# Three small moves of order and engine in a one-core decoder layer: a turn's copies, a unit's scores, a round's sums of weights

## The chip, the cores and the metric

The kernel runs on one core of a Trainium2 chip. The metric is the device time of one execution in microseconds (us). In the text PE is TensorE, DVE is VectorE, ACT is ScalarE, POOL is GpSimd, and SP is the engine that issues most DMAs. PEld stands for the loads of weights into PE, which overlap its products. L705 is line 705 of the kernel before.

## The reference

One decoder layer over 512 tokens of width 1024, in fp32:

```python
x = x + 0.5 * swiglu(rms_norm(x, g_ffn1), w_ffn1_gate, w_ffn1_up, w_ffn1_down)
proj = rms_norm(x, g_mix) @ w_in             # q, k, v, conv input u, memory queries mq
y_attn = sliding_window_attention(...)       # 8 heads, window 128, per-head sinks
y_conv = conformer_conv(...)                 # GLU, causal depthwise conv of 31 taps, LayerNorm, swish
y_mem  = memory_cross_attention(...)         # 4 heads into 256 memory tokens
x = x + concat(y_attn, y_conv, y_mem) @ w_out
x = x + 0.5 * swiglu(rms_norm(x, g_ffn2), w_ffn2_gate, w_ffn2_up, w_ffn2_down)
```

with `swiglu(x, wg, wu, wd) = (silu(x @ wg) * (x @ wu)) @ wd` and 2816 hidden columns.

## The kernel before

Activations lie transposed, channels on the 128 partitions and the 512 tokens along the free axis. Every product with weights is made of three products of parts in fp32r: high times high, low times high, high times low. So each weight tile is loaded as fp32 by SP (`wraw`), split into a high part by an ACT cast (L208, L214) and a low part by a DVE subtraction (L209, L219). The class `Weights` keeps that queue in order: `split_to(n)` makes all items up to n, `four(i)` makes the sums of one weight tile.

The layer has three stages: the first feed-forward block (to about 360 us), the mixing stage with attention, convolution and memory (to about 510 us), and the second feed-forward block. Most of the feed-forward products use a seven-product scheme (Strassen-Winograd) on halves of 256 tokens, which needs sums of weight blocks: `four` computes four sums of 128x256 each with four DVE instructions (L147 to L150).

**Mixing.** The steps are written in a list, `ORDER`. The six attention units are M0, M1 (memory) and S0 to S3 (window), each of two heads. For each unit: `scores?0` and `scores?1` (products of q and k into two `sc` or two `mm` banks of PSUM, L1161), `soft?j` (masked maxima on DVE, L1179, exponentials on ACT, L1197), `weights?` (division by the sums, split over DVE, L1217, and ACT, L1219), `turn?h` (for a window unit seven PE transposes, L1232, in groups of four and three into two `tp` banks, and a copy of each group to SBUF, L1235, by ACT), and `values?` (L1246), whose result is split into yh and yl (L1262, L1263). `c` is one pair of convolution taps on DVE (L1089). `out{d}_{ks}` adds products of the output projection for column block d (L421 to L423). `ln_mean`, `ln_square` and `ln_var` are the LayerNorm of the convolution (L1351 to L1376), `ln_swish` its end (L1382, L1383). A planner orders the instructions of each engine from modelled times, with the order of the program as priority; on the chip each engine then works through its own order and waits where an operand isn't there. There are four `mm`, two `sc` and two `tp` banks, handed out as they come free.

**Last down round.** It is the one stage in which PE, DVE and ACT keep the order of the program exactly. `seven(g)` does columns 2g and 2g+1 of the output for g = 0 to 3, with two weight items each: `wa` (the raw tile, three quarters) and `ws` (the four sums). The halves of results are taken from PSUM by ACT (`half`, L530), added into x (by a POOL DMA with accumulation for g = 0, L590, by DVE from there on, L588) and the finished columns are written by `leave` (L598: one DVE operation, then an output DMA, L601). `leave` for quarter g runs in quarter g+1. `ahead` prepares the weights of the next quarters. For g < 2 it is called after the product T1, for g > 1 at the beginning of the quarter. For g = 1 it makes the second item of quarter 2 and the sums for quarter 3.

Of the kernel before, what the change touches and what calls it, by code (L numbers as in the profile page):

```python
# [67 lines left out]
pS0 ropeS0 pS1 sumA facA ropeS1 c valuesM1 pS2 scoresS01 scoresS00 softS00 softS01 c weightsS0 ropeS2 c  # L68
pS3 scoresS10 softS10 scoresS11 out0_01 sumB facB c turnS00 turnS01 softS11 scoresS20 c weightsS1 c c
valuesS0 turnS10 scoresS21 out1_01 softS20 out1_2 ropeS3 softS21 c c turnS11 weightsS2 c valuesS1 scoresS30  # L70
turnS20 out0_2 scoresS31 softS31 turnS21 softS30 out1_3 out2_0123 weightsS3 c c out0_3 valuesS2 c c out3_0123 c
c ln_mean ln_square turnS30 ln_var out4_0123 turnS31 out5_0123 valuesS3
""".split()
TILES = [s[1:] for s in ORDER if s[0] == "p"]
# [202 lines left out]
def layer(tc, ctx, a):  # L277
    nc = tc.nc
    PE, ACT, DVE, POOL = nc.tensor, nc.scalar, nc.vector, nc.gpsimd
# [12 lines left out]
    def mm_bank():  # L292
        return psum.tile([P, T], F32, tag="mm", name=nm("mm"), bufs=4)

    def sc_bank():
        return psum.tile([P, T], F32, tag="sc", name=nm("sc"), bufs=2)
# [4 lines left out]
    def work():  # L301
        return tmp.tile([P, T], F32, tag="t", name=nm("t"), bufs=5)
# [5 lines left out]
    W = Weights(nc, wpool, dma_ahead=3, conv_ahead=3, bufs=(4, 4))  # L308
# [53 lines left out]
    def atile(name, dtype=F32R):  # L362
        i = turns["n"] = (turns["n"] + 1) % (N_ACT + 1)
        if turns["more"] and i == N_ACT:
            return tmp.tile([P, T], dtype, tag="sqsum", name=nm(name), bufs=1)
        return act.tile([P, T], dtype, tag="h", name=nm(name), bufs=N_ACT)
# [101 lines left out]
    def ffn(pool, norm, first, gain, hooks, next_gain, last):  # L468
# [52 lines left out]
        def product7(ps, w, at, step, block, first, n):  # L521
            for q in range(2):
                hi, lo = sevens[n][q][block]
                s = slice(at + q * step, at + q * step + P)
                PE.matmul(ps, w[0][:, s], hi, start=first and q == 0, stop=False, skip_group_check=not first)  # L525
                PE.matmul(ps, w[0][:, s], lo, start=False, stop=False, skip_group_check=not first)  # L526
                PE.matmul(ps, w[1][:, s], hi, start=False, stop=q == 1, skip_group_check=not first)  # L527

        def half(to, ps, sign=1):
            ACT.activation(to, ps, AF.Copy, scale=0.5 * sign)  # L530

        def twice(ps):
            return ps.unsqueeze(1).to_broadcast([P, 2, 256])
# [40 lines left out]
        def seven(g):  # L574

            l, r = slice(0, 256), slice(256, 512)
            end = g == 3
            bank = tp_bank if g == 2 else mm_bank
            b, de, c = bank()[:, l], bank(), sc_bank()[:, l]
            s12, s45 = (kept(), work()) if end else (atile("s12", F32), atile("s45", F32))  # L580
            x0, x1 = x[:, 2 * g], x[:, 2 * g + 1]

            def prod(*args):
                product7(*args, plan.last)

            def add(to, part):
                if g > 0:
                    DVE.tensor_tensor(to, to, part, op=ALU.add)  # L588
                else:
                    POOL.dma_start(to, part, accum_op=ALU.add)  # L590

            def leave(d, t, ps):
                o = work()[:, : t.stop - t.start]
                xd = x[:, d, t]
                if ps.shape[-1] < t.stop - t.start:
                    o, xd = (v.rearrange("p (a b) -> p a b", a=2) for v in (o, xd))
                    ps = twice(ps)
                DVE.scalar_tensor_tensor(o, ps, 0.5, xd, op0=ALU.mult, op1=ALU.add)  # L598
                if len(o.shape) == 3:
                    o = o.rearrange("p a b -> p (a b)")  # L600
                nc.sync.dma_start(a["out"][d, :, t], o)  # L601

            def ahead():
                W.split_to(at + 4)
                if g < 2:
                    W.four(W.items[at + 4][0])

            at = W.at
            if g > 1:
                ahead()  # L610
            wa, ws = W.next(), W.next()
            whole = slice(0, T)
            e = bank()[:, l] if end else de[:, l]

            def p2():
                prod(e, wa, 128, 256, H_21, True)

            def p4():
                prod(c, wa, 512, 128, H_T4, True)
                half(s45[:, l], c, -1)  # L620
                add(x1, s45)

            def p3():
                prod(de[:, r], ws, 768, 128, H_22, False)

            def p7():
                prod(b, ws, 512, 128, H_T3, False)

            prod(b, wa, 0, 256, H_11, True)
            half(s12[:, l], b)  # L630
            if not end:
                p2()
            prod(de[:, r], ws, 0, 128, H_T1, True)
            half(s45[:, r], de[:, r])
            if g < 2:
                ahead()
            while later:
                leave(*later.pop(0))
            if end:
                p4()  # L640
            prod(b, ws, 256, 128, H_T2, False)
            half(s12[:, r], b)
            add(x0, s12)
            if not end:
                p4()
                W.split_to(W.at + 3)
                p3()
                p7()
                later.extend([(2 * g + 1, whole, b), (2 * g, whole, de)])
                return  # L650
            p2()
            leave(2 * g, l, e)
            p7()
            leave(2 * g + 1, whole, b)
            p3()
            leave(2 * g, r, de[:, r])
# [9 lines left out]
        def kept():  # L666
            return pool.tile([P, T], F32, tag="kept", name=nm("kept"), bufs=3)
# [123 lines left out]
        for f in range(NF):  # L791
# [10 lines left out]
            else:  # L802
                g, u = (sc_bank(), sc_bank()) if f % 3 == 2 else (mm_bank(), mm_bank())
# [209 lines left out]
    for c in range(4):  # L1013
        f = MEM_F - 2 + (c + 1) // 2
# [16 lines left out]
def mixing(tc, nc, a, mix, W, norm, e):  # L1031
    PE, ACT, DVE, POOL = nc.tensor, nc.scalar, nc.vector, nc.gpsimd
# [29 lines left out]
    def pttile():  # L1062
        return mix.tile([P, T], F32, tag="pt", name=nm("pt"), bufs=8)
# [30 lines left out]
    def pump(n):  # L1094
        for _ in range(n):
            next(tap, None)
# [35 lines left out]
    def rope(q):  # L1132
        s = work()
        u = work()
        DVE.stream_shuffle(s, q, list(range(8, 16)) + list(range(0, 8)) + list(range(16, 32)))
        DVE.tensor_tensor(s, s, sinb, op=ALU.mult)
        DVE.tensor_tensor(u, q, cosb, op=ALU.mult)
        DVE.tensor_tensor(q, u, s, op=ALU.add)


    class Attend:
# [76 lines left out]
                    else:  # L1218
                        ACT.activation(self.p[n, h][:, c], self.p[n, h][:, c], AF.Copy, scale=self.den[:, i : i + 1])  # L1219

        def turn(self, h):

            if self.win:
                slots = [(0, 0), (1, 0), (1, 1), (2, 1), (2, 2), (3, 2), (3, 3)]
                groups = [slots[:4], slots[4:]]
            else:
                groups = [[(n, b) for n in range(NB)] for b in range(2)]
            for g in groups:
                ps = tp_bank()
                for i, (n, b) in enumerate(g):  # L1230
                    c = (b - n + 1) * P if self.win else b * P
                    PE.transpose(ps[:, i * P : (i + 1) * P], self.p[n, h][:, c : c + P], ident)  # L1232
                s = pttile()
                w = len(g) * P
                ACT.copy(s[:, :w], ps[:, :w])  # L1235
                for i, (n, b) in enumerate(g):
                    self.pt[h, n, b] = (s, i)

# [42 lines left out]
    v = {}  # L1281
# [13 lines left out]
    def sums(name, *tiles):  # L1295
        v["st" + name] = head_sums([v["sq" + t] for t in tiles])
# [81 lines left out]
    def ln_swish():  # L1378
# [8 lines left out]
    steps = {  # L1387
        "sumM": lambda: sums("M", "M0", "M1"), "facM": lambda: factors("M", "M0", "M1"),
        "sumA": lambda: sums("A", "S0", "S1"), "facA": lambda: factors("A", "S0", "S1"),
        "sumB": lambda: sums("B", "S2", "S3"), "facB": lambda: factors("B", "S2", "S3"),  # L1390
        "sumK": lambda: sums("K", "K"), "facK": key_factor, "normK": key_norm, "turnV": value_turn,
        "ropeK": lambda: rope(kT), "c": lambda: pump(1),
        "ln_mean": ln_mean, "ln_square": ln_square, "ln_var": ln_var,
    }
    for t in TILES:
        steps["p" + t] = lambda t=t: project(t)
    for t, y in units.items():
        if t[0] == "S":
            steps["rope" + t] = lambda t=t: rope(v[t])
        for j in range(2):  # L1400
            steps[f"scores{t}{j}"] = lambda t=t, j=j: v["at" + t].scores(j)
            steps[f"soft{t}{j}"] = lambda t=t, j=j: v["at" + t].soft(j)
            steps[f"turn{t}{j}"] = lambda t=t, j=j: v["at" + t].turn(j)
        steps["weights" + t] = lambda t=t: v["at" + t].weights()
        steps["values" + t] = lambda t=t, y=y: v["at" + t].values(y)
    for d in range(6):
# [112 lines left out]
```

## Time and profile before

| | |
|---|---|
| median of 3 runs | 850.5 us (849.34, 850.50, 851.39) |
| the profiled execution: time, span | 851.12 us, 849.3 us |
| granted clock of PE | 0.997 of full |
| PE busy | 838.5 us (99%) |
| DVE busy | 755.1 us (89%) |
| ACT busy | 530.3 us (62%) |
| POOL busy | 101.3 us (12%) |

The profile is one execution, and times in it count from the start of its span. The device time of that execution is a little longer than its span. A busy share is an average over the whole span; what a step costs has to be read from the stage in which it stands.

### The profile page before, as it was taken

To read this page: it belongs to the slowest core of one execution; us is meant where nothing else is said; L and a number is where in the kernel's file an instruction comes from. 1 tells how busy PE (TensorE), PEld (TensorE's weight loads), DVE (VectorE), ACT (ScalarE), POOL (GpSimd) and SP (SyncE) were. 2 spreads that over 40 slices of the span, in tenths; PEclk is the share of its full clock that TensorE was granted. 3 is DMA by queue.
4 is the path that set the end of the run, shared out by engine and by line. 5 is a ranking of instruction groups with operands and counts; after the bars stand their busy time and mean duration, and the time that the engine had idled before them with its cause. 6 is when DMAs were issued, how large, how long until landed. Compare 5 with 4: busy or idle time off the path is not lost. (4 is left out here: it accounts for less than half of the span.)

```text
span 849.3 us, 16223 instructions
## 1 busy us (share of the span) xinstructions
PE 838.5 (99%) x6277; PEld 776.8 (91%) x6277; DVE 755.1 (89%) x1385; ACT 530.3 (62%) x999; POOL 101.3 (12%) x114
## 2 busy tenths in 40 slices
PE   8999999999999999999999999999999999999997
PEld 5889999999999999988676788889999999999996
DVE  7998999998888897959988985799988999999997
ACT  7465567776764444533948764656555677768773
POOL 0010002132110000400000021220000121313111
PEclk9999999999999999999999999999999999999999
DMA  7435338778773334222001332873334677887755
GB/s 277 125 89 140 98 123 193 181 183 209 188 188 118 123 110 133 76 98 63 14 28 36 90 100 86 198 151 106 116 112 108 161 175 183 198 190 163 191 125 150
DMA packets 47454, 114.56 MB, mean 135 GB/s; under 512 B 4624, under 2 KB 9232, under 8 KB 47376
## 3 DMA queue, kind: packets, MB, share of 16 engines
q1 hardware_dynamic: 32032, 85.99, 32.4%
q0 software_dynamic: 14192, 25.96, 18.2%
q10 hardware_dynamic: 1152, 1.57, 0.6%
q8 instruction: 49, 0.80, 0.4%
q14 instruction: 29, 0.24, 0.1%
HBM read 88.07 MB, written 2.10 MB: 106 GB/s over the span
## 5 line engine op out<-in xcount | busy, mean ns | idle before, releaser
L705 PE MATMUL mm<-bh,w 128*128 128x256 f32 x888 | 245.8, 277 | 0.5 <-ACT kept L724 0.5
L706 PE MATMUL mm<-bl,w 128*128 128x256 f32 x888 | 245.3, 276 | 0.0
L707 PE MATMUL mm<-bh,w 128*128 128x256 f32 x888 | 245.2, 276 | 0.0
L705 PEld LDWEIGHTS mm<-bh,w 128*128 128x128 f32 x888 | 166.7, 188 | 1.2 <-ACT kept L724 1.1
L706 PEld LDWEIGHTS mm<-bl,w 128*128 128x128 f32 x888 | 166.7, 188 | 0.1
L707 PEld LDWEIGHTS mm<-bh,w 128*128 128x128 f32 x888 | 166.7, 188 | 0.0
L214 ACT CAST w<-wraw 128x1024 fp32r<-128x1024 f32 (+2 forms) x99 | 98.3, 998 | 64.0 <-issue 26.4
L219 DVE TENSOR_TENSOR w<-wraw,w 128x1024 fp32r<-128x1024 f32 (+2 forms) x93 | 108.4, 1167 | 9.7 <-ACT w L214 8.6
L219 DVE TENSOR_TENSOR w<-s,w 128x1024 fp32r<-128x1024 f32 x61 | 74.5, 1222 | 15.7 <-ACT w L214 14.4
L422 PE MATMUL mm<-hl,w 128*128 128x256 f32 (+1 forms) x264 | 79.2, 301 | 0.0
L423 PE MATMUL mm<-hh,w 128*128 128x256 f32 (+1 forms) x264 | 79.1, 300 | 0.0
L421 PE MATMUL mm<-hh,w 128*128 128x256 f32 (+1 forms) x264 | 78.5, 301 | 0.0
L214 ACT CAST w<-s 128x1024 fp32r<-128x1024 f32 x61 | 64.0, 1049 | 19.6 <-PE mm L707 9.4
L525 PE MATMUL mm<-h,w 128*128 128x256 f32 x258 | 71.6, 278 | 0.1
L527 PE MATMUL mm<-h,w 128*128 128x256 f32 x258 | 71.2, 276 | 0.0
L526 PE MATMUL mm<-h,w 128*128 128x256 f32 x258 | 71.2, 276 | 0.0
L421 PE MATMUL mm<-xh,w 128*128 128x512 f32 x176 | 69.7, 401 | 1.0 <-ACT w L230 1.0
L422 PE MATMUL mm<-xl,w 128*128 128x512 f32 x176 | 69.4, 394 | 0.5 <-DVE xl L433 0.5
L423 PE MATMUL mm<-xh,w 128*128 128x512 f32 x176 | 69.0, 392 | 0.0
L735 ACT ACTIVATE t<-t 128x512 f32<-128x512 f32 x37 | 23.4, 633 | 49.3 <-DVE t L734 49.1
L422 PEld LDWEIGHTS mm<-hl,w 128*128 128x128 f32 x264 | 49.5, 188 | 2.5 <-DVE hl L664 0.2
L421 PEld LDWEIGHTS mm<-hh,w 128*128 128x128 f32 x264 | 49.4, 188 | 2.4 <-ACT hh L663 0.3
(327 smaller groups left out, 2101.5 us busy)
## 6 DMA issues: line engine op xcount, KB each, us to landing
wraw<-in_wgu SPq DMA_DIRECT2D x86, 512.0 KB, 3.6
wraw<-in_wd SPq DMA_DIRECT2D x38, 512.0 KB, 3.9
wraw<-in_win SPq DMA_DIRECT2D x12, 512.0 KB, 3.5
x<-cosb POOLq DMA_DIRECT2D x18, 256.0 KB, 3.3
x<-sinb POOLq DMA_DIRECT2D x18, 256.0 KB, 3.6
x<-mk POOLq DMA_DIRECT2D x18, 256.0 KB, 5.4
x<-mv POOLq DMA_DIRECT2D x18, 256.0 KB, 5.6
x<-t POOLq DMA_DIRECT2D x12, 256.0 KB, 4.2
```

What stands on the lines that cost most here:

```text
L214: nc.scalar.copy(hi[:, :cols], raw[:, :cols])
L219: nc.vector.tensor_tensor(lo[:, :cols], raw[:, :cols], hi[:, :cols].bitcast(F32), op=ALU.subtract)
L421: PE.matmul(ps[:, t], wh[:, w], hi(k)[:, t], start=one, stop=False, skip_group_check=cut > 1)
L422: PE.matmul(ps[:, t], wh[:, w], lo(k)[:, t], start=False, stop=False, skip_group_check=cut > 1)
L423: PE.matmul(ps[:, t], wl[:, w], hi(k)[:, t], start=False, stop=end, skip_group_check=cut > 1)
L525: PE.matmul(ps, w[0][:, s], hi, start=first and q == 0, stop=False, skip_group_check=not first)
L526: PE.matmul(ps, w[0][:, s], lo, start=False, stop=False, skip_group_check=not first)
L527: PE.matmul(ps, w[1][:, s], hi, start=False, stop=q == 1, skip_group_check=not first)
L705: PE.matmul(ps, wh[:, c], bh[k][:, block], start=one, stop=False, skip_group_check=not first)
L706: PE.matmul(ps, wh[:, c], bl[k][:, block], start=False, stop=False, skip_group_check=not first)
L707: PE.matmul(ps, wl[:, c], bh[k][:, block], start=False, stop=end, skip_group_check=not first)
L735: ACT.activation(g, g, AF.Silu)
```

## The change

Three edits. In `ORDER`, `scoresS31` stands before `turnS20` and `out0_2` instead of after them. In `turn`, the copy from PSUM is done by the function passed in, and turnS11 alone is given `DVE.tensor_copy`, so its two copies move from ACT to DVE. In `seven`'s `ahead`, the sums for quarter g+2 are made before `split_to` when g is 1, and after it, as before, when g is 0.

```diff
-turnS20 out0_2 scoresS31 softS31 turnS21 softS30 out1_3 out2_0123 weightsS3 c c out0_3 valuesS2 c c out3_0123 c
+scoresS31 turnS20 out0_2 softS31 turnS21 softS30 out1_3 out2_0123 weightsS3 c c out0_3 valuesS2 c c out3_0123 c
...
             def ahead():
+                if g == 1:
+                    W.four(W.items[at + 4][0])
                 W.split_to(at + 4)
-                if g < 2:
+                if g < 1:
                     W.four(W.items[at + 4][0])
...
-        def turn(self, h):
+        def turn(self, h, copy=ACT.copy):
...
-                ACT.copy(s[:, :w], ps[:, :w])
+                copy(s[:, :w], ps[:, :w])
...
-            steps[f"turn{t}{j}"] = lambda t=t, j=j: v["at" + t].turn(j)
+            steps[f"turn{t}{j}"] = lambda t=t, j=j: v["at" + t].turn(j, *[DVE.tensor_copy] * (t + str(j) == "S11"))
```

## Rows read from the trace of the kernel before

**Rows 1.** The page's busy times of the engines over the whole span.

```profile
PE 838.5 (99%) x6277; PEld 776.8 (91%) x6277; DVE 755.1 (89%) x1385; ACT 530.3 (62%) x999; POOL 101.3 (12%) x114
```

**Rows 2.** Busy time of each engine by stretch of the span: the stretch, its length, then busy us and (instructions) of PE, PEld, DVE, ACT and POOL, then the granted clock, the DMA share and GB/s.

```profile
460.00:480.00 20.00, 19.03 (x138) 14.33 (x137) 18.49 (x59) 18.53 (x55) 0.00 (x0) 1.00 0.10 28
480.00:500.00 20.00, 19.55 (x118) 15.64 (x117) 16.25 (x35) 12.88 (x21) 0.00 (x0) 1.00 0.39 119
500.00:800.00 300.00, 299.82 (x2347) 287.84 (x2346) 271.77 (x439) 195.81 (x355) 52.22 (x56) 1.00 0.62 151
800.00:849.30 49.30, 43.37 (x377) 42.83 (x375) 43.48 (x78) 27.89 (x61) 7.59 (x9) 0.98 0.57 142
835.00:846.00 11.00, 8.37 (x71) 7.97 (x69) 10.81 (x18) 3.92 (x9) 0.00 (x0) 1.00 0.39 146
```

**Rows 3.** The timeline around S3's second scores, of PE, DVE and ACT: start, us, engine, line, operation, out<-in, count [idle before <-releaser].

```profile
462.95 0.50 PE L421 MATMUL mm<-yh,w 128*128 128x512 f32 x1
463.29 0.93 PE L1232 MATMUL tp<-ident,p 128*128 128x128 f32 x7
463.97 0.47 PE L422 MATMUL mm<-yl,w 128*128 128x512 f32 x1
...
464.61 1.13 PE L1161 MATMUL mm<-kT,q 64*128 64x256 f32 x8
466.71 0.50 PE L421 MATMUL mm<-yh,w 128*128 128x512 f32 x1 [0.97 <-DVE s L1179]
...
467.85 1.75 PE L1246 MATMUL tp<-pt,vtok 128*64 128x128 f32 x28
...
460.78 0.42 DVE L1179 CUSTOM_DVE_ANT_0 p<-mm,mask 128x256 f32<-128x256 f32 x1
...
465.88 0.42 DVE L1179 CUSTOM_DVE_ANT_0 p<-mm,mask 128x256 f32<-128x256 f32 x1 [1.13 <-PE mm L1161]
...
466.95 0.94 ACT L1235 COPY pt<-tp 128x512 f32<-128x512 f32 x2
```

**Rows 4.** DVE instructions of one line each, over the whole span: count, least/median/most ns, first and last start, forms.

```profile
L1376 DVE COPY t<-s x1: 427/427/427, 493.4 to 493.4; 128x512 f32<-128x512 f32 x1
...
L1263 DVE TENSOR_TENSOR yl<-tp,yh x6: 683/684/692, 421.7 to 495.4; 128x512 fp32r<-128x512 f32 x6
```

**Rows 5.** The timeline from the last taps to the end of the LayerNorm, of DVE, of PE and PEld.

```profile
475.72 0.69 DVE L219 TENSOR_TENSOR w<-wraw,w 128x512 fp32r<-128x512 f32 x1 [0.31 <-ACT w L214]
...
489.44 0.68 DVE L1363 TENSOR_TENSOR t<-t,t 128x512 f32<-128x512 f32 x1
...
498.37 0.69 DVE L1263 TENSOR_TENSOR yl<-conv,yh 128x512 fp32r<-128x512 f32 x1 [0.68 <-ACT yh L1262]
...
490.18 0.97 PEld L1370 LDWEIGHTS tp<-ones,t 128*128 128x128 f32 x8 [0.25 <-DVE t L1363]
...
499.07 0.39 PE L421 MATMUL mm<-yh,w 128*128 128x512 f32 x1
...
499.97 0.39 PE L422 MATMUL mm<-yl,w 128*128 128x512 f32 x1
```

**Rows 6.** The timeline of the last down round: the loads of its weights on SP's queue (first issue, us to the last, five loads), and DVE.

```profile
796.98 16.61 SPq L178 DMA_DIRECT2D wraw<-in_wd  x5
...
827.35 1.23 DVE L219 TENSOR_TENSOR w<-s,w 128x1024 fp32r<-128x1024 f32 x1
...
830.08 1.02 DVE L209 TENSOR_TENSOR w<-wraw,w 128x512 fp32r<-128x512 f32 x2
832.11 1.23 DVE L219 TENSOR_TENSOR w<-s,w 128x1024 fp32r<-128x1024 f32 x1 [1.00 <-ACT w L214]
833.25 0.42 DVE L147 TENSOR_TENSOR s<-wraw 128x256 f32<-128x256 f32 x1
...
834.50 0.42 DVE L150 TENSOR_TENSOR s<-wraw 128x256 f32<-128x256 f32 x1
835.00 1.29 DVE L598 SCALAR_TENSOR_TENSOR t<-mm,x 128x512 f32<-128x512 f32 x2
```

**Rows 7.** The same round on ACT and on PE.

```profile
835.03 1.05 ACT L214 CAST w<-s 128x1024 fp32r<-128x1024 f32 x1 [1.59 <-DVE s L150]
835.98 0.65 ACT L530 ACTIVATE s<-tp 128x256 f32<-128x256 f32 x2
...
833.16 0.28 PE L527 MATMUL mm<-bh,w 128*128 128x256 f32 x1
...
834.86 0.28 PE L527 MATMUL tp<-h,w 128*128 128x256 f32 x1
...
...
836.41 0.39 PE L525 MATMUL tp<-h,w 128*128 128x256 f32 x1 [0.94 <-ACT s L530]
...
844.03 0.28 PE L527 MATMUL mm<-bh,w 128*128 128x256 f32 x1
```

**Rows 8.** The chain that ended last, in order of time: start, us, what.

```profile
843.35 1.20 DVE x L588 x2
...
845.66 0.33 DVE t L598
```

**Rows 9.** POOL's transfers that add quarter 0's halves into x: durations of issue in ns, first and last start, and their time to landing in us.

```profile
L590 POOL DMA_DIRECT2D x<-s x2: 1487/1660/1834, 828.4 to 829.0; - x2
...
DMA to landing us min/median/max: 5.2/5.6/6.0
```

## The prediction

> **What bounds the kernel now.** I read the page's busy times first. PE is busy 99% of the span, DVE 89% and ACT 62% [rows 1]: TensorE sets the pace unless a stage says otherwise, so the change has to be priced by stage. The table of stretches says where PE is not full [rows 2]: it loses 0.97 us between 460 and 480, 0.45 between 480 and 500, 0.2 in the 300 us after that, and 5.9 in the last 49, most of it behind its last product. The edits lie in the first and in the last of these. The timeline names one stall in each: 0.97 us in a product of line 421 behind a mask read of line 1179 [rows 3], and 0.94 us in a product of line 525 behind a copy of line 530 [rows 7]. All else that PE does is work which no part of the change removes. So the most that can be had is about 0.97 + 0.94 = 1.9 us, if both stalls vanish and nothing else ends later. Last I read the chain that ended last: its end is VectorE's, not PE's [rows 8].
>
> **The attention, before.** The seven transposes of turnS11 run at 463.29, the second scores of S3 (eight products of line 1161) at 464.61 to 465.74; then PE stands until 466.71, because out2 needs one of the `mm` banks that hold these scores [rows 3]. VectorE had run out of planned work too: it waits 1.13 us for those scores and reads the masks from 465.88 [rows 3]. ScalarE is in a long row of exponentials and comes to turnS11's two copies only at 466.95; valuesS1 starts at 467.85, when the first is there [rows 3].
>
> **Moving scoresS31.** Nothing is added; eight products change place with the three of out0_2 and with turnS20 (whose inputs weightsS2 makes only later, so that it does not matter). What it passes is out0_2's three products, which hold PE from 462.95 to 463.29 and from 463.97 to 464.61 [rows 3]: 0.34 + 0.64 us. So the scores come 0.6 to 1.0 us earlier, and out0_2 later by their 1.13. Nobody waits for out0_2 alone: it only adds into a bank that out0_3 needs again much later. The masks can then be read at about 465.0 rather than 465.88, out2's bank comes free earlier, and out0_2 is work for PE in the hole. The 0.97 us stall should go.
>
> **Moving turnS11's copies.** ScalarE loses two copies; the pair takes 0.94 us [rows 3]. VectorE gains one copy of 128x512 and one of 128x384 from PSUM. No such copy of VectorE is in the trace. Bounds: a VectorE copy of 512 columns from SBUF is 0.43 us, its two-operand operations on 512 columns from the same `tp` banks 0.68 [rows 4]. With the narrow one scaled by 384/512 the pair costs between 0.75 and 1.19 us; I take 1.19, as the source bank is the nearer likeness, and keep 0.75 for the range. The cover is the 1.13 us in which VectorE idles [rows 3]: earlier scores take the idle time away, the copies fill it, so VectorE is 1.19 - 1.13 = 0.06 us later at 466, or nothing. Without that cover it is later by the whole 1.19. The gain is that valuesS1 can run at about 466 instead of 467.85, again in PE's hole, and that ScalarE reaches weightsS2 some 0.9 us sooner, so that turnS20 and valuesS2 come forward as well.
>
> Is VectorE the engine to give this work to? Between 460 and 480 it is busy 18.49 us of 20 and ScalarE 18.53 [rows 2], so on this row neither is the one with room. [...]
>
> **What the early gain meets.** From 466 to 490 VectorE hardly pauses (the longest pause is 0.31 us, before 475.72 [rows 5]). Its convolution taps end in ln_mean, the squares and their sum at 489.44 to 490.12, and PE's ln_var products at 490.18 already stand 0.25 us for that sum [rows 5]. If VectorE is no earlier, a PE that is 0.97 us earlier meets this wait and gives all of it back, unless the plan puts other products in front of ln_var. There are some: turnS31's transposes and valuesS3 come behind it in the list. Past that point the LayerNorm chain has room: its last low part starts at 498.37 and ends about 499.06, and PE asks for it in the fifth product after 499.07, at 499.97 [rows 5]: 0.9 us to spare. So the gain that is left at 500 lies between nothing and 0.97, plus the waits of 0.25 and 0.31 if ScalarE's relief reaches them. I take 0.6, a little above the middle. From 500 to 800 PE is busy for 299.8 of 300 us [rows 2], so it is carried through.
>
> **The last down round.** The sums for quarter 3 (four VectorE adds, 833.25 to 834.92) move ahead of quarter 2's second low part (line 219, 1.23 us), in front of which VectorE waits 1.00 us for ScalarE's cast [rows 6]. No instruction is added and no DMA is moved: the last of the round's loads was issued by 813.6, and the buffer of the sums was last read at 827.35 [rows 6]. After: sums from 831.10 to 832.77, low part from there to 833.95. PE wants this low part at 834.86 [rows 7], 0.9 us later, so no new stall. ScalarE now waits 1.59 us for the sums and casts them at 835.03; only then comes the halving at 835.98, and for that PE stands 0.94 us, to 836.41 [rows 7]. After: cast at about 833.45, when PE is through with the buffer (its last product there starts at 833.16 [rows 7]), halving at 834.5, and PE goes on at 835.47 without a stall.
>
> But who ends last there? VectorE starts line 598 at 835.00 [rows 6], is busy for 10.81 of the 11.00 us from there [rows 2], and ends with line 598 at 845.66 + 0.33 = 845.99 [rows 8]. PE's last product ends at 844.31 [rows 7]. So it is VectorE's row that has to start sooner, and what starts it is not the sums alone. Line 598 reads column block 1 of x, into which POOL's transfer of line 590 adds; the second of the two transfers starts at 829.0 and takes the longer time in its row, 6.0 us, to land: at 835.0 [rows 9], the moment at which line 598 starts. That transfer depends on quarter 0 alone and isn't touched. So VectorE will be through with sums and low part at 833.95 and wait 1.0 us for the landing: the wait moves from one place to another, and the 11 us behind it stay. I take 0 for this part. The other bound is 0.94, if the landing does not bind; for a loss the low part would have to slip by over 0.9 us.
>
> [...]
>
> **Sum.** The profiled execution took 851.12 us with a span of 849.3, so 1.8 lies outside the span; it stands 0.6 above the 850.5 median of three runs that reach from 849.34 to 851.39. 849.3 - 0.6 - 0 gives a span of 848.7 and 850.5 for such an execution; on the median it is 850.5 - 0.6 = 849.9.
>
> **Rivals.**
> Both stalls are worth their length: 850.5 - 0.97 - 0.94 = 848.6. For it: PE is at 99%. Against: the landing at 835.0 and VectorE's unbroken row. It needs the landing at least 0.9 us sooner. Chance 0.2.
> Nothing is left: PE meets ln_var early and waits there; tail as said: 850.5. For it: the 0.25 us wait that is there already. Chance 0.25.
> Slower: VectorE works in the planned order, and a copy that stands ahead of the taps holds them until its transposes are there. That such a plan goes wrong by about a us is seen in the 1.13 us before the masks. If the copies stand right behind S2's masks (which end at 461.2) while the transposes end at 464.2 [rows 3], VectorE loses up to 3.0 us and pays 1.19 for the copies, less the 1.13 idle: ln_mean comes up to 3.1 later, and beyond the 0.9 us of room PE waits: up to +2.2, 852.7; the middle is +1.0, 851.5. It decides as soon as VectorE is over 0.9 us late at 485. Chance 0.15.
> The forecast, 849.9 with its own range of 849.3 to 850.4, has the other 0.4.
>
> A difference of 0.2%, 1.7 us, is about what a measurement of this kernel tells from none. Faster by more: the first rival, and a small part of the forecast for the order of the plan, which can shift more than these steps: 0.25. Slower by more: the last third or so of the slower rival, and the same allowance: 0.09. Within: 0.66. The range: 848.6 to 851.5 takes in the first rival and the middle of the slower.
>
> **What would show it.** Right: line 1235's copies are 22 on ScalarE and 2 on VectorE at about 0.68 and 0.5 us; no wait of line 421 behind line 1179 of 1 us; in the tail no wait of PE in line 525, but a new wait of about 1 us of VectorE in front of the first line 598, whose start stays some 11 us before VectorE's end. Wrong: that line 598 starts a us sooner relative to the last low part of the round before (then the landing did not bind); VectorE waits for turnS11's transposes; or PE's wait at ln_var grows to 1 us or more.

## The result, and the profile after

The changed kernel takes 856.41 us (median of six executions, 853.45 to 858.02) against 850.56 for the kernel before on the same chip: a ratio of 1.0063, interval 1.0049 to 1.0077. It is slower by some 5.5 us, above the range of the prediction, where a gain was forecast. The profiled execution took 853.45 us with a span of 851.7. It is the quickest of the six and had the highest granted clock, 0.998; the other five had 0.992 to 0.996. So this profile shows less than the typical loss, which matters below.

The busy times on the page after; nothing in them tells the loss [rows 1]:

```profile
PE 839.5 (99%) x6277; PEld 777.8 (91%) x6277; DVE 755.8 (89%) x1387; ACT 528.6 (62%) x997; POOL 101.4 (12%) x114
```

The table of stretches of the kernel after, all engines' busy us, then the granted clock:

```profile
460.00:480.00 20.00, 19.90 (x140) 15.31 (x140) 18.94 (x57) 17.98 (x53) 0.00 (x0) 1.00 0.19 54
480.00:500.00 20.00, 17.00 (x98) 13.47 (x97) 14.21 (x31) 9.20 (x15) 0.00 (x0) 0.91 0.30 93
490.00:500.00 10.00, 8.60 (x60) 7.32 (x61) 5.53 (x18) 5.38 (x10) 0.00 (x0) 0.83 0.10 39
```

Against [rows 2]: between 460 and 480 PE loses 0.10 us where it lost 0.97, as forecast. Between 480 and 500 it loses 3.0 where it lost 0.45, and the granted clock there is 0.91; in the second half of that stretch it is 0.83. The largest wait of PE, from the table of waits:

```profile
PE tp L1372 <- DVE t L1365: 2.3, 1, 2.3
```

That is ln_var (line 1370 before) waiting for VectorE's sum of squares. The timeline of the kernel after, PE's, VectorE's and ScalarE's rows around it:

```profile
454.24 1.75 PE L1248 MATMUL tp<-pt,vtok 128*64 128x128 f32 x28
463.57 1.75 PE L1248 MATMUL tp<-pt,vtok 128*64 128x128 f32 x28
...
485.93 1.02 PE L1355 MATMUL tp<-t,t 128*128 128x512 f32 x2
...
487.45 0.40 PE L423 MATMUL sc<-yh,w 128*128 128x512 f32 x1
...
490.95 1.05 PE L1372 MATMUL tp<-ones,t 128*128 128x1 f32 x8 [2.34 <-DVE t L1365]
...
493.17 3.24 PE L1248 MATMUL tp<-pt,vtok 128*64 128x128 f32 x28 [0.35 <-ACT pt L1237]
...
462.29 1.16 DVE L1237 COPY pt<-tp 128x512 f32<-128x512 f32 x2 [0.21 <-PE tp L1234]
465.82 0.17 DVE L1212 TENSOR_TENSOR den<-den,s 128x8 f32<-128x8 f32 x1 [0.63 <-ACT s L1211]
475.69 0.17 DVE L1212 TENSOR_TENSOR den<-den,s 128x8 f32<-128x8 f32 x1 [0.22 <-ACT s L1211]
...
484.53 0.69 DVE L1353 TENSOR_TENSOR t<-conv 128x512 f32<-128x512 f32 x1
485.13 2.36 DVE L219 TENSOR_TENSOR w<-wraw,w 128x1024 fp32r<-128x1024 f32 x2
487.40 1.28 DVE L1357 TENSOR_TENSOR conv<-conv,tp 128x512 f32<-128x512 f32 x2
490.20 0.69 DVE L1365 TENSOR_TENSOR t<-t,t 128x512 f32<-128x512 f32 x1 [1.52 <-ACT t L1363]
...
487.42 0.58 ACT L1237 COPY pt<-tp 128x512 f32<-128x512 f32 x1 [3.87 <-PE tp L1234]
488.64 0.48 ACT L1237 COPY pt<-tp 128x384 f32<-128x384 f32 x1 [0.64 <-PE tp L1234]
489.02 1.15 ACT L1363 ACTIVATE t<-conv 128x512 f32<-128x512 f32 x2
```

Two things are to be seen. PE stands 2.34 us at 490.95. And behind the stall the 28 products of valuesS3, at 493.17, take 3.24 us, where the same 28 products take 1.75 at 454.24 and 463.57: there TensorE runs at half of its clock, a granted 0.50 in each microsecond from 493 to 496. Over 490 to 500 the mean clock is 0.83, so (1 - 0.83) x 2 x 10 = 3.4 us of it were at half speed.

The tail, VectorE's rows of the timeline after, PE's one wait, and the last row of the chain that ended last:

```profile
834.97 1.22 DVE L219 TENSOR_TENSOR w<-s,w 128x1024 fp32r<-128x1024 f32 x1
837.34 1.29 DVE L598 SCALAR_TENSOR_TENSOR t<-mm,x 128x512 f32<-128x512 f32 x2 [1.15 <-DMA x<-s]
...
841.96 0.39 PE L527 MATMUL mm<-h,w 128*128 128x256 f32 x1 [0.49 <-DVE w L219]
...
847.99 0.33 DVE t L598
```

VectorE waits 1.15 us for the landing of the transfer of line 590 where it waited 1.00 for the cast before [rows 6], and from the first line 598 to the end it takes 847.99 + 0.33 - 837.34 = 10.98 us. Before it was 10.99 [rows 6, 8].

### The profile page after: what moved, and what is told of

Same layout as the page of the kernel before. It is cut to its first block, busy times and chain, and to the rows that moved or that the text cites. A ratio compares the mean times of both kernels' runs of the same rounds, so it can differ in the third digit from the quotient of the medians.

```text
span 851.7 us, 16222 instructions
## 1 busy us (share of the span) xinstructions
PE 839.5 (99%) x6277; PEld 777.8 (91%) x6277; DVE 755.8 (89%) x1387; ACT 528.6 (62%) x997; POOL 101.4 (12%) x114
```

## The experiments

Twelve runs, in three groups; the kernels of a group share their runs of the kernel before, whose medians were 850.73, 850.68 and 851.01. Intervals are those of the ratio to it.

### The three edits one by one

**e1_tail**: the kernel before with the edit of `ahead` alone.

```diff
+                if g == 1:
+                    W.four(W.items[at + 4][0])
                 W.split_to(at + 4)
-                if g < 2:
+                if g < 1:
```

> The kernel before with the last edit alone: quarter 3's sums ahead of quarter 2's second low part. Theory A (the landing of GpSimd's transfer starts VectorE's last row): no change, 850.5 within 0.6; PE's 0.94 us stall at line 525 is gone, VectorE waits 1.0 to 1.2 us for the landing in front of the first line 598, and 11.0 us lie between that start and VectorE's end, as before. Rival (PE's stall is worth its length): 849.6.

Measured: 850.36 us, ratio 0.9999 (0.9987 to 1.0011). The tail edit is worth nothing that this interval of about 1 us to either side can tell, and costs nothing.

**e2_copies**: the kernel before with turnS11's two copies on VectorE alone.

```diff
-                ACT.copy(s[:, :w], ps[:, :w])
+                copy(s[:, :w], ps[:, :w])      # DVE.tensor_copy for turnS11 alone
```

> The kernel before with turnS11's two copies on VectorE alone. Theory A (the copies bring PE ahead, it spends the output products before ln_mean, and the plan puts ScalarE's second copy of turnS30 in front of the squares, so that ln_var's sum is about 0.8 us later, PE stands over 2 us there and its clock falls to half behind that): most of the loss of the whole change, 853 to 857, with a PE wait at ln_var of 1.5 to 2.5 us. Rival B (the scores' move is what does it): 850 to 851. Rival C (VectorE pays 1.2 us for the copies and nothing else): 851.7, the wait at ln_var near 1.2 and the clock full.

Measured: 856.61 us, ratio 1.0063 (1.0038 to 1.0088). This edit alone has the whole loss. PE's largest wait and the values of S3 in its timeline:

```profile
493.23 1.86 PE L1370 MATMUL tp<-ones,t 128*128 128x1 f32 x8 [2.34 <-DVE t L1363]
496.73 3.25 PE L1246 MATMUL tp<-pt,vtok 128*64 128x128 f32 x28
```

**e3_scores**: the kernel before with scoresS31 written sooner alone.

```diff
-turnS20 out0_2 scoresS31 softS31 ...
+scoresS31 turnS20 out0_2 softS31 ...
```

> The kernel before with scoresS31 moved alone. Theory A: the order of ScalarE around the squares is that of before, so the sum is not late; the 0.97 us stall behind the masks is gone and some of it is kept: 849.6 to 850.5. Rival B (the scores' move does the harm): 853 or more.

Measured: 850.46 us, ratio 0.9995 (0.9984 to 1.0006). PE's 0.97 us stall is gone, yet valuesS1 now waits 0.75 for its copies, and nothing is gained that can be measured: another wait of the same engine took the place of the first.

**e4_after**: the whole change again, on the chip of the three.

> The changed kernel again, for a second profile of it and its clock. Its first profiled run had the shortest time of six. Theory A with the clock: 855 to 857 at the median; a mean granted clock under 0.997, and more than one stretch at half clock between 485 and 510 us of the span when the run is slower than 853.5. Rival (the longer runs wait longer at ln_var, with the clock as in the first profile): the PE wait there is 4 us or more.

Measured: 855.85 us, ratio 1.0061 (1.0041 to 1.0082). In its profiled execution, too, the stall at the variance is 2.34 us; the mean clock over 490 to 500 is 0.83, one stretch of 3.4 us at half clock behind the stall and not more. The second stretch that was expected of any execution above 853.5 us is not in this one of 854.71 us; e2_copies has it (last section).

So the loss has to be sought in the copies, and the intervals show no part of it that is an interplay of the three.

### The stall, the order and the clock

**f1_warm**: the changed kernel with two products that nothing uses put into the stall.

```diff
+        for _ in range(2):
+            PE.matmul(vs, ident, conv[:, 0], start=True, stop=True)
         for b in range(NB):
             PE.matmul(vs[:, b : b + 1], ...
```

> The changed kernel with two more fp32 products of TensorE (identity times one half of the convolution's tile, 0.85 us apart by the product of the mean) put ahead of the variance's products, into the bank that these then overwrite: the results don't use them. They fill some 1.7 us of the 2.34 us in which TensorE stood at the variance and delay nothing else, as VectorE's sum is not touched. Theory 'late sum and half clock': the loss is some 2.2 us of lateness and the rest a halved clock behind the stall; with TensorE kept busy the rows behind 491 show the full clock, the values of the last unit take 1.75 us and not 3.24, and the time is 852.5 to 854 (changed kernel 856). Rival 'the clock falls by itself, whatever TensorE does' : half clock again in the stretch 490 to 500 and 855.5 to 856.5. Rival 'the extra products cost': above 856.5.

Measured: 852.75 us, ratio 1.0022 (1.0009 to 1.0034), so some 3.1 us less than the changed kernel in e4_after; the intervals of the two ratios don't overlap. Its timeline: the two unused products (line 1372, two records each), the variance, the values.

```profile
489.36 1.98 PE L1372 MATMUL tp<-conv,ident 128*128 128x512 f32 x4 [0.57 <-ACT pt L1237]
491.29 0.95 PE L1374 MATMUL tp<-ones,t 128*128 128x1 f32 x8
493.31 1.75 PE L1248 MATMUL tp<-pt,vtok 128*64 128x128 f32 x28 [0.26 <-ACT pt L1237]
```

The variance and the values start no sooner than in the changed kernel (the one 0.14 us later, the other 0.06 sooner, counted from the start of valuesS0), the useful work is the same, and yet 3.1 us are back: they are the clock's. The 2.1 us that remain are as much as the lateness itself. The other executions agree: the mean granted clock over the ten of f1_warm is 0.9984 and over the 31 of the kernel before beside them 0.9983, while the four of e4_after have 0.9940.

**f2_order**: the changed kernel with turnS30 behind ln_var in `ORDER`.

```diff
-c ln_mean ln_square turnS30 ln_var out4_0123 ...
+c ln_mean ln_square ln_var turnS30 out4_0123 ...
```

> The changed kernel with one step moved in the written order: the last unit's first turn stands behind the variance's products and no longer ahead of them, so ScalarE squares ahead of that turn's two copies and TensorE turns behind the variance. Theory 'the stall is made at three queues': ScalarE's squares come 0.46 us earlier at least, and the turn's seven transposes no longer stand ahead, so that the sum comes some 0.5 to 0.9 us earlier; but TensorE now has 1.2 us of transposes less to do ahead of the variance, so its stall there is as long or longer (2.3 to 3 us), with the half clock behind it: 855 to 856.5. Rival 'ScalarE's order alone makes the stall': stall under 1 us and 851 to 852.

Measured: 855.2 us, ratio 1.0050 (1.0037 to 1.0062). The sum came 0.8 us sooner, but PE had the turn's transposes no longer to do ahead of the variance and stood 2.80 us; the mean clock was 0.96 over 480 to 490 and 0.70 over 490 to 500, so it was at half for 6.8 us together. So ScalarE's order alone is not what makes the stall.

```profile
489.67 1.84 PE L1372 MATMUL tp<-ones,t 128*128 128x1 f32 x8 [2.80 <-DVE t L1365]
```

**f3_act**: the changed kernel with the last unit's scaling by ScalarE alone.

```diff
-ON_DVE = [(0,), (1, 3), (1, 3), (2, 3), (1, 3), (1, 3)]
+ON_DVE = [(0,), (1, 3), (1, 3), (2, 3), (1, 3), ()]
```

> The changed kernel with VectorE's share of the last unit's scaling by the softmax's sums (two instructions, some 1.1 us together, at 477) given to ScalarE: VectorE then does as much as before the change ahead of the LayerNorm. Theory 'VectorE's lateness': the add of the LayerNorm's mean goes from 484.5 to some 483.5, the sum from 490.2 to some 489, TensorE's stall at the variance from 2.3 to 1.2 us or less, and half clock behind it less often: 851 to 853. Rival 'TensorE is ahead, VectorE is not late': the sum is at 490 as before, the stall of 2.3 us stays: 855.5 to 856.5. Rival 'ScalarE is now late': its waits ahead of the turns of the last unit grow, and the time is 855 or more.

Measured: 853.6 us, ratio 1.0025 (1.0011 to 1.0040). About half of the loss is gone, less than was expected (851 to 853). The stall at the variance is 1.64 us still, more than the 1.2 expected: VectorE's arrival was put right, the sum only in part (table below).

```profile
491.53 1.06 PE L1372 MATMUL tp<-ones,t 128*128 128x1 f32 x8 [1.64 <-DVE t L1365]
```

**f6_extra**: the kernel before, with the two copies done by VectorE once more into tiles that nothing reads.

```diff
                 ACT.copy(s[:, :w], ps[:, :w])
+                if more:                      # turnS11 alone
+                    DVE.tensor_copy(work()[:, :w], ps[:, :w])
```

> The kernel before with its ScalarE copies as they are, and on VectorE the same two copies done once more into work tiles that nothing reads: VectorE has the 1.16 us of work, ScalarE keeps its own, and nothing comes sooner for TensorE. Theory 'VectorE's time alone carries the loss': sum and variance late by about 1 us, a stall at the variance of 1 us or more, and 853 to 856. Rival 'it takes TensorE being ahead': TensorE still has products left at the variance, the stall stays under 0.5 us, and 850.4 to 851.5.

Measured: 855.35 us, ratio 1.0047 (1.0032 to 1.0062); one of its ten executions took 2170.67 us and is left out of the ratio (the median of the other nine is 855.13). In its timeline:

```profile
467.42 1.16 DVE L1237 COPY t<-tp 128x512 f32<-128x512 f32 x2
492.35 1.05 PE L1372 MATMUL tp<-ones,t 128*128 128x1 f32 x8 [2.10 <-DVE t L1365]
```

Here nothing came sooner for PE (valuesS1 starts 13.18 us behind valuesS0 where it was 12.17), ScalarE had all its copies still, and the stall and the loss are there. The rival that PE has to be ahead falls: 1.16 us more of VectorE ahead of the LayerNorm are enough.

### How much VectorE's arrival weighs, and the tail

**h2_one**: the kernel before with the narrow copy of the two on VectorE.

```diff
-                ACT.copy(s[:, :w], ps[:, :w])
+                (small if w < T else ACT.copy)(s[:, :w], ps[:, :w])
```

> The kernel before with one of the two copies alone on VectorE, the narrow one (128x384, 0.55 us in the changed kernel); the other stays on ScalarE. Theory 'a threshold': VectorE comes 0.3 us later to the LayerNorm's mean (0.55 less the 0.27 us of idle time that the pair took up), TensorE's stall at the variance stays under 0.8 us, the clock stays whole behind it, and the time is 850.5 to 851.5. Rival 'in proportion': 0.55 of 1.16 us gives 0.47 of the loss of 5.2 us, 853 to 853.5. Rival 'the plan's order turns over with the least delay' (two low parts ahead of the subtraction of the mean, a copy ahead of the squares): stall of 1.5 us or more and 853 to 856.

Measured: 854.37 us, ratio 1.0032 (1.0018 to 1.0046); stall at the variance 1.41 us. The threshold of 0.9 us falls: VectorE was 0.36 us late at the LayerNorm's add, and the loss was about half of the whole. Nearest is the reading by which the order turns over with the least delay; its stall of 1.5 us was just missed.

**f4_act**: the kernel before with the edit of f3_act.

> The kernel before with VectorE's share of the last unit's scaling (1.1 us) given to ScalarE: the opposite of the copies, VectorE has less to do ahead of the LayerNorm. Theory 'VectorE's arrival at the LayerNorm sets TensorE's wait at the variance': the sum comes 0.5 to 1 us sooner and the wait of 0.25 us there is gone, but there is no more to win than this: 850.0 to 850.7. Rival 'ScalarE pays for it' (the last unit's turns wait for the scaling): 851 to 853.

Measured: 851.68 us, ratio 1.0008 (0.9998 to 1.0018): nothing won. Against the expectation the sum came no sooner, though VectorE came 1.08 us sooner to the add (table below). No cost to ScalarE's turns is seen either: valuesS3 starts 36.71 us behind valuesS0, as before 36.72. VectorE and valuesS0 in its timeline:

```profile
456.09 1.75 PE L1246 MATMUL tp<-pt,vtok 128*64 128x128 f32 x28
...
484.43 0.68 DVE L1351 TENSOR_TENSOR t<-conv 128x512 f32<-128x512 f32 x1
485.03 2.36 DVE L219 TENSOR_TENSOR w<-wraw,w 128x1024 fp32r<-128x1024 f32 x2
487.30 1.28 DVE L1355 TENSOR_TENSOR conv<-conv,tp 128x512 f32<-128x512 f32 x2
489.83 0.69 DVE L1363 TENSOR_TENSOR t<-t,t 128x512 f32<-128x512 f32 x1 [1.25 <-ACT t L1361]
```

**h1_swap**: e1_tail with quarter 0's two columns leaving in the other order, so that the one that landed first goes first.

```diff
-                later.extend([(2 * g + 1, whole, b), (2 * g, whole, de)])
+                later.extend([(2 * g, whole, de), (2 * g + 1, whole, b)] if g == 0 else [...])
```

> The kernel before with the tail edit and, in the last round's first quarter, the two columns that leave in quarter 1 taken in the other order, so that the column whose transfer was issued first and landed after 5.2 us goes first and the one of 6.0 us second. Theory 'the landing holds the tail': VectorE starts its first operation of line 598 some 1.1 us sooner, waits some 0.5 us for the second, and its end comes 0.5 to 0.7 us sooner: 850.0 against 850.7. Rival 'something else holds the tail': the wait moves again and the time is that of the kernel before.

Measured: 851.26 us, ratio 0.9996 (0.9986 to 1.0005). The first line 598 no longer waits and the second does, for the same landing:

```profile
834.75 0.69 DVE L598 SCALAR_TENSOR_TENSOR t<-mm,x 128x512 f32<-128x512 f32 x1
836.07 0.69 DVE L598 SCALAR_TENSOR_TENSOR t<-mm,x 128x512 f32<-128x512 f32 x1 [0.63 <-DMA x<-s]
```

That the landing holds VectorE is shown. From the start of the low part ahead of line 598 to VectorE's end it takes 846.45 - 833.62 = 12.83 us, in e1_tail 844.49 - 831.13 = 13.36: the 0.5 us that were expected are in the trace, but too little for the median to show.

**h3_best**: the scores and the tail edits, the edit of f3_act and that of h1_swap, without the copies.

> The change without its copies (the scores and the tail edits), with the last unit's scaling all on ScalarE and with the two leaving columns of the run above in the other order. If VectorE's arrival at the LayerNorm is what takes the gain of the scores back, 0.5 to 1 us of the removed stall of 0.97 us is kept now, and with 0.6 us from the tail the time is 849 to 849.8. Rival 'the earlier TensorE meets another wait': 850 to 850.7. Rival 'ScalarE is late': above 851.

Measured: 850.77 us, ratio 0.9994 (0.9985 to 1.0004), so the gain that was expected did not come. No version was found that beats the kernel before by more than the measurement tells.

## Why the prediction was wrong

**What held.** The tail: nothing for the end, a wait of 1.15 us for the landing where 1.0 was written, 10.98 us from there. (A wait of PE of 0.49 us for the next low part came new and costs nothing: VectorE ends last.) The copies: 1.16 us the pair where 1.19 was taken, 692 and 548 ns, 22 others left on ScalarE. PE's 0.97 us stall is gone, and valuesS1 starts 9.33 us behind valuesS0 where it was 12.17. One of the prediction's signs of being wrong came too: "PE's wait at ln_var grows to 1 us or more".

**The step that failed first** is "the copies fill it, so VectorE is 1.19 - 1.13 = 0.06 us later at 466, or nothing". The idle time was not filled; it moved. VectorE's waits between valuesS0 and the LayerNorm in e1_tail, whose mixing stage is that of before:

```profile
464.47 0.42 DVE L1181 CUSTOM_DVE_ANT_0 p<-mm,mask 128x256 f32<-128x256 f32 x1 [1.04 <-PE mm L1163]
474.28 0.69 DVE L219 TENSOR_TENSOR w<-wraw,w 128x512 fp32r<-128x512 f32 x1 [0.29 <-ACT w L214]
```

They are 1.33 us; after the change they are 0.21 + 0.63 + 0.22 = 1.06 (rows above). Of 1.16 us of copies only 0.27 was covered, so VectorE should come 0.89 us later to the LayerNorm's add; counted from valuesS0 it comes 0.82 later than in e1_tail and 0.87 later than in the profile of the kernel before. Two new waits for ScalarE's exponentials of the sinks (line 1211) took the place of the one for the masks. The first of these operands did come some 0.8 us sooner, as ScalarE had no copies ahead of it, but VectorE's order asked for it sooner still. Both engines were at 18.5 of 20 us here [rows 2]. e2_copies, with the copies alone, is slower by a ratio of 1.0063.

**The second step that failed** is the room: "past that point the LayerNorm chain has room: ... 0.9 us to spare". That room was read at the chain's last low part, at 499. The place that decides is ln_var, ten microseconds ahead, and there VectorE's sum was already the last thing to come [rows 5]. The rival for a slower kernel set its point of decision at "over 0.9 us late", and h2_one pays at 0.36; its mechanism, copies that hold the taps until the transposes are there, came to 0.21 us only (the copies' row above).

**The third thing was in no step.** The delay grows between the add and the sum, because the planner's order at the LayerNorm turned over. Times of the traces, in us counted from the start of valuesS0 of the same execution (after: 484.53 - 454.24 = 30.29):

| kernel | VectorE's add | PE's mean | subtraction | squares | sum | stall at the variance | valuesS3 starts | ratio |
|---|---|---|---|---|---|---|---|---|
| before | 29.42 | 30.36 | 31.42 | 32.34 | 33.76 | none | 36.72 | 1 |
| f4_act | 28.34 | 29.42 | 31.21 | 32.55 | 33.74 | none | 36.71 | 1.0008 |
| f3_act | 29.12 | 30.43 | 31.99 | 33.57 | 34.75 | 1.64 | 38.19 | 1.0025 |
| h2_one | 29.78 | 31.00 | 32.66 | 34.13 | 35.31 | 1.41 | 38.28 | 1.0032 |
| f6_extra | 30.36 | 31.82 | 33.23 | 34.95 | 36.14 | 2.10 | 39.10 | 1.0047 |
| after | 30.29 | 31.69 | 33.16 | 34.78 | 35.96 | 2.34 | 38.93 | 1.0063 |

The kernel before, at valuesS0, VectorE's add and valuesS3:

```profile
455.68 1.75 PE L1246 MATMUL tp<-pt,vtok 128*64 128x128 f32 x28
485.10 0.69 DVE L1351 TENSOR_TENSOR t<-conv 128x512 f32<-128x512 f32 x1
492.40 1.75 PE L1246 MATMUL tp<-pt,vtok 128*64 128x128 f32 x28 [0.35 <-ACT pt L1235]
```

In the kernel before the sum comes 4.34 us after the add; in all the others of the table it is 5.4 to 5.8. The rows of e1_tail, whose order here is that of before:

```profile
483.66 0.70 DVE L1353 TENSOR_TENSOR t<-conv 128x512 f32<-128x512 f32 x1
484.26 1.23 DVE L219 TENSOR_TENSOR w<-wraw,w 128x1024 fp32r<-128x1024 f32 x1
485.67 1.28 DVE L1357 TENSOR_TENSOR conv<-conv,tp 128x512 f32<-128x512 f32 x2 [0.18 <-PE tp L1355]
486.87 1.22 DVE L219 TENSOR_TENSOR w<-wraw,w 128x1024 fp32r<-128x1024 f32 x1
488.01 0.69 DVE L1365 TENSOR_TENSOR t<-t,t 128x512 f32<-128x512 f32 x1
...
486.11 0.59 ACT L1237 COPY pt<-tp 128x512 f32<-128x512 f32 x1 [1.79 <-PE tp L1234]
486.59 1.16 ACT L1363 ACTIVATE t<-conv 128x512 f32<-128x512 f32 x2
487.64 0.47 ACT L1237 COPY pt<-tp 128x384 f32<-128x384 f32 x1
```

There the subtraction of the mean stands between the two low parts, and ScalarE's squares between turnS30's two copies. After the change both low parts go ahead of the subtraction and both copies ahead of the squares (first timeline), and PE's mean starts 0.71 us after the add is over instead of 0.25, as more output products stand ahead of it. The other four changed kernels of the table have VectorE and ScalarE in this second order too. The sum is 35.96 - 33.76 = 2.20 us late: 0.87 is VectorE's arrival, 0.46 PE's mean, 0.41 VectorE's low part, and 0.46 the rest up to the sum, mostly ScalarE's second copy. f3_act shows the order nearly by itself: VectorE comes 0.30 us sooner than before, yet the sum is 0.99 late. f4_act bears this out from the other side: VectorE comes 1.08 us sooner, the order turns over all the same, and the sum is where it was. So over half of the lateness goes with the order, and the order of the kernel before was a good one that each of the five changes of VectorE's load, more or less, lost.

**The fourth, in the typical execution of the changed kernel the largest, was in no step either: the clock.** The profile after against e1_tail: span 851.7 - 847.8 = 3.9, of which 38.93 - 36.78 = 2.15 us is valuesS3 starting later (36.78 is e1_tail's) and 3.24 - 1.75 = 1.5 the half clock; 0.25 is spread. In the typical execution the clock costs twice that: f1_warm, in which TensorE has work in the stall, stands 2.1 us above the kernel before, as much as the lateness; the changed kernel stood 5.1 above it (e4_after), so 3.0 us are the clock's, give or take 2 by the two intervals. The mean granted clocks of the executions give a second, rough estimate of the clock's part: what a kernel's mean lacks against that of the kernel before beside it, times 850 us.

| kernel | valuesS3 later, us | clock's part, estimate | sum | loss by the ratio |
|---|---|---|---|---|
| e4_after | 2.2 | 3.8 | 6.0 | 5.2 |
| f6_extra | 2.4 | 1.0 | 3.4 | 4.0 |
| f3_act | 1.5 | 0.8 | 2.3 | 2.1 |
| h2_one | 1.6 | 0.6 | 2.1 | 2.7 |
| f1_warm | 2.1 | -0.1 | 2.0 | 1.9 |

The two terms come within 1 us of the loss of each kernel; in f6_extra, f3_act and h2_one the lateness is the larger. Within one kernel the clock does not order the executions: in e4_after one of 856.74 us had 0.996 and one of 855.75 had 0.992.

What is open: why the plan turns over (its modelled times are not in the traces); what the order costs with all else equal, as no run has the copies together with the old order; and how much of f4_act's missing gain lies there rather than behind 500.

## What to carry to other kernels

Idle time of an engine is no cover until it is known what ends it and what the next operand waits for: compare an engine's arrival at the next fixed point, not the hole. Read the room where the delayed result is awaited with nothing else to do (here the variance, not the end of the chain). Where a planner orders the engines, an edit of one us can turn an order some twenty us behind it, so a forecast should carry that in its range on the slower side, and a stall of TensorE of some 2 us should be priced with the half clock that can follow it, not by its length: here 3.4 or 6.8 us at half clock with a stall of 2.34 us, and none in f6_extra with 2.10.

## What the runs showed of the hardware

In the profiles of five runs with stalls of 1.64 to 2.80 us at the variance the granted clock of TensorE fell to half, by its means over ten microseconds for 3.4 us (0.83: f3_act with a stall of 1.64, the changed kernel and e4_after with 2.34) or 6.8 (e2_copies with 2.34, f2_order with 2.80). The stretch from 490 to 500 in e1_tail (no stall) and in f1_warm (stall filled), in this order; the column before the last two is the clock:

```profile
490.00:500.00 10.00, 9.55 (x67) 7.77 (x66) 7.56 (x21) 6.01 (x9) 0.00 (x0) 1.00 0.18 46
```

```profile
490.00:500.00 10.00, 9.65 (x70) 7.37 (x69) 6.21 (x19) 6.91 (x11) 0.00 (x0) 1.00 0.13 48
```

After the change it is 0.83 (first table), in e2_copies it is 0.66:

```profile
490.00:500.00 10.00, 7.63 (x49) 6.31 (x48) 3.92 (x16) 4.37 (x8) 0.00 (x0) 0.66 0.28 100
```

It does not follow every time: f6_extra's profiled execution stood 2.10 us and kept the whole clock, 1.00 over 490 to 500, and so did h2_one's with 1.41 us. So the length of the stall alone does not tell whether the clock falls. f6_extra:

```profile
490.00:500.00 10.00, 7.45 (x62) 6.03 (x61) 5.52 (x18) 6.83 (x12) 0.00 (x0) 1.00 0.21 86
```

And the kernel before has such a stretch in its own profile, with a clock of 0.50 from 452 to 454, without a stall of TensorE near it, between 450 and 460, where it has scores, transposes and values to do and few wide products:

```profile
450.00:460.00 10.00, 10.00 (x69) 7.30 (x67) 8.95 (x49) 8.01 (x26) 0.00 (x0) 0.83 0.11 28
```

e1_tail's profile has none there (1.00 over 450 to 460), and reaches valuesS0 at 454.19 rather than 455.68. Of these 1.49 us 0.19 were there already at 444.9, so this stretch alone is 1.3 us of the spread from one execution to the next. What brings the fall about is not shown. Every stall at the variance was shorter than the time at half clock that came with it, where any came: 2.80 us at the longest and 2.34 in the changed kernel, against 3.4 or 6.8. Between the product at 487.45 and valuesS3 at 493.17 the changed kernel has only transposes and products of one column around the stall, and no run here tells whether they have a part in it.
